# A hybrid decoder layer on one core: the first FFN's first part leaves raw, operand sums move to POOL, and a block's down products go behind

## The chip, the cores and the metric

One Trainium2 chip, one of its cores. The metric is the device time of one execution in microseconds, the median over runs. TensorE (PE) multiplies and has a separate loader of weights (PEld); VectorE (DVE), ScalarE (ACT) and GpSimd (POOL) do the elementwise work; SyncE (SP) issues nearly all DMAs. TensorE's clock has two levels, 1.2 and 2.4 GHz, and the profile shows what was granted (PEclk, 1.00 is 2.4 GHz).

## The reference, cut to what matters

One decoder layer over 1024 prompt tokens and 64 sample tokens, 1088 columns in all. The change touches the first FFN:

```
rmsnorm(x, g) = x * rsqrt(mean(x*x) + 1e-6) * g
swiglu(x)     = (silu(x @ w_gate) * (x @ w_up)) @ w_down      # 1024 -> 2752 -> 1024
h = x + 0.5 * rmsnorm(swiglu(rmsnorm(x, g1)), g2)
u = rmsnorm(h, g3)          # then the projection u @ w_in, attention, a second FFN
```

## The kernel before, in words

**Layout and precision.** Features lie on the 128 partitions (8 blocks of 128 for 1024), tokens in columns. Every operand of TensorE is split into a high part (rounded by ScalarE, `split`, L194) and a low part (the rest, by VectorE, L195), and each product is three matmuls: high by high, high by low, low by high. FFN rows come in 22 blocks of 128, block 0 a half block (the tail). `GROUPS` (L30) makes 7 groups of them: [0,1], four of four blocks, [18,19] and [20,21].

**Two parts.** The first FFN runs as `f1a` over columns 0 to 511 and then `f1b` over 512 to 1087 (576 columns, chunks of 256 and 320). A part goes through the groups in order (`plan1`, L1653): group 0 by `job_first` (L520), groups 1 to 5 as "sevens", group 6 plain ("final"). After a group's gate and up products, four jobs (`job_down`, L637) multiply its hidden blocks by a quarter each of `w_down` and add the result into `y` (L511; the first group copies, L509).

**Sevens** (`seven`, `job_seven`, `sevens`). For a hidden block, gate and up together are a two by two block product over halves of the features and halves of the columns, done with seven products of half size instead of eight. It needs sums of weight blocks (`Sums.load`, L77, on POOL, with scratch) and sums of operand blocks: `sevens` (L620) subtracts quarters of the normalised `y` in place on VectorE (L630, eight subtracts), and splits each into operands. For `f1a` the scratch of the weight sums and of the products is `y1`, for `f1b` it is `y0`; the operand sums' splits lie in the other part's operand tiles (`flata`, `flatb`). Since `sevens` works in place in `y`, group 0's down products wait, in order of issue, for all of it (`need`, L640), before the tail weights `wt` are cast (L643, L644).

**End of a part.** Group 6's down jobs run by chunks and square each row block as it is finished (`square`, L269). `f.after` then starts `norm` (L351): statistics by a matmul with ones (L294), rows by a matmul with a diagonal (L343), eight scalar_tensor_tensors (L382), the residual added (L383) and the result stored to `h1`, squares again, statistics again, eight scalar_tensor_tensors for the next norm (L405). For `f1b` the result is split into operands (L411, L412). For `f1a` it is stored in DRAM as `u0` (`spill`, L408), because `y0` must become scratch; `olds` of `f1b` begins with `need(("u0", ...))` (L1662), and `next2` (L1648), after `f1b`'s sevens, has `again` (L1637) load `u0` into `y0` and split it. The projection's first unit needs it (`hook2`, L1674).

**What sets the order.** Jobs are issued in one list (`work`, L694); `Feed` (L98) loads weights two requests ahead and splits up to three ahead (`NW`). Work beside TensorE's is a generator; `tick` (L210), called after each few matmuls with their estimated time, steps `quick` and the first of `side`. The framework's scheduler then reorders instructions within each engine by readiness in its own model, except where `keep` asks for program order.

Of the kernel before, what the change touches and what calls it, by code (L numbers as in the profile page):

```python
# [8 lines left out]
F32 = mybir.dt.float32  # L9
# [4 lines left out]
ALU = mybir.AluOpType  # L14
# [4 lines left out]
P = 128  # L19
D = 1024  # L20
KB = 8
# [136 lines left out]
class Part:  # L158
# [4 lines left out]
    room = None  # L163


class Step:
# [184 lines left out]
    def norm(self, y, y0, c0, n, pool, post=None, pre=None, v=None, key=None, spill=None):  # L351
# [49 lines left out]
        for k in range(KB):  # L401
# [4 lines left out]
            if spill is not None:  # L406
                if k % 4 == 3:
                    nc.sync.dma_start(spill[:, k - 3:k + 1, c0:c0 + n], y[:, k - 3:k + 1, c0 - y0:c0 - y0 + n])  # L408
                continue
# [5 lines left out]
    def ffn(self, w_gu, w_dn, f):  # L415
# [64 lines left out]
        def down(g, d2, w, wt, c0, n, first, s0=0, sums=None):  # L480
            hi, lo = w
            o = slice(c0 - f.b0, c0 - f.b0 + n)
            pds = {}
            seq = []
            for part in ((g[:-1], g[-1:]) if len(g) > 1 else (g,)):
                for e in range(2):
                    for hb in part:
                        i = g.index(hb)
                        hh, hl = hid[hb]
                        s = slice(s0 + (2 * i + e) * P, s0 + (2 * i + e) * P + P)  # L490
                        x, xl = hh[:, o], hl[:, o]
                        if hb == HB_TAIL:
                            ops = [(wt[:, e * P:e * P + P], x), (hi[:, s], xl)]
                        else:
                            ops = [(hi[:, s], x), (hi[:, s], xl), (lo[:, s], x)]
                        seq.append((e, i, ops))
            for e, i, ops in seq:
                if e not in pds:
                    pds[e] = self.mm(n)
                for j, (a, b) in enumerate(ops):  # L500
                    nc.tensor.matmul(pds[e], a, b, start=(i == 0 and j == 0), stop=(i == len(g) - 1 and j == len(ops) - 1))  # L501
                self.tick(len(ops) * n * COL)

            def evac():
                for e in range(2):
                    k = 2 * d2 + e
                    yk = f.y[:, k, c0 - f.y0:c0 - f.y0 + n]
# [4 lines left out]
                    if sums is not None:  # L512
                        self.square(yk, k, n, f.N, sums)
# [1364 lines left out]
```

## Time and profile before

| what | value |
|---|---|
| median of 3 runs | 2407.62 us (2406.84 to 2412.11) |
| the profiled execution | 2410.29 us, its span 2408.5 us, mean granted clock 0.976 |
| PE busy | 2270.2 us (94%) |
| PEld busy | 2039.4 us (85%) |
| DVE busy | 1616.2 us (67%) |
| ACT busy | 1041.9 us (43%) |
| POOL busy | 693.6 us (29%) |
| DMA | 362.71 MB, 151 GB/s over the span |

The chain of waits that ended last goes mostly through TensorE's matmuls (17% of the span by its rows). Matmuls overlap, so a mean duration is longer than the step from one to the next; the step is read from a stretch's instructions and its length. Times are microseconds from the start of the span.

### The profile page before, as it was taken

Reading aid. Unit: us, or ns where it says so; the run is one execution under the profiler, and the core shown is the slowest. Engines: PE = TensorE matmul, PEld = TensorE weight load, DVE = VectorE, ACT = ScalarE, POOL = GpSimd, SP = SyncE. Lnnn points to the kernel's source line nnn. Section 1 sums busy time; section 2 is a strip of 40 time slices with the busy share of each in tenths; the row PEclk is TensorE's granted clock in tenths of the full one; section 3 lists DMA queues with packets and bytes.
Section 4 is the critical chain, followed back from the end, with each engine's and each line's share of the span. In section 5 each row is a group of like instructions: output and inputs, shape, how many; then the busy total and the mean of one; then the engine's idle time right before and its main releaser. Section 6 shows DMA issues by size and latency. Waiting matters only on the chain. (4 is left out here: it accounts for less than half of the span.)

```text
span 2408.5 us, 41672 instructions
## 1 busy us (share of the span) xinstructions
PE 2270.2 (94%) x15584; PEld 2039.4 (85%) x15584; DVE 1616.2 (67%) x2881; ACT 1041.9 (43%) x1786; POOL 693.6 (29%) x650
## 2 busy tenths in 40 slices
PE   6999999699999999999999999998997999999997
PEld 5888978699999978989998566667786988999997
DVE  6887868678776575676556233339785696778765
ACT  5444335334433355665454222226465644344332
POOL 3444413333441021011125453631010224334402
PEclk8999999799999999999999999999998999999998
DMA  4332332533222367665356998865555545333212
GB/s 140 110 95 93 91 126 63 168 94 98 87 87 82 108 205 242 208 197 160 116 185 207 334 315 295 298 185 161 165 165 158 176 133 162 101 93 94 80 58 91
DMA packets 203627, 362.71 MB, mean 151 GB/s; under 512 B 28257, under 2 KB 103842, under 8 KB 203426
## 3 DMA queue, kind: packets, MB, share of 16 engines
q1 hardware_dynamic: 191762, 321.76, 42.8%
q0 software_dynamic: 11664, 38.28, 4.6%
q8 instruction: 124, 2.03, 0.3%
q14 instruction: 77, 0.63, 0.1%
HBM read 314.17 MB, written 45.79 MB: 149 GB/s over the span
## 5 line engine op out<-in xcount | busy, mean ns | idle before, releaser
L265 PE MATMUL mm<-ua,wh 128*128 128x512 f32 (+2 forms) x1712 | 461.8, 358 | 9.1 <-ACT wh L194 5.8
L195 DVE TENSOR_TENSOR wl<-wr,wh 128x1024 fp32r<-128x1024 f32 (+1 forms) x249 | 290.6, 1167 | 145.7 <-ACT wh L194 136.9
L194 ACT CAST wh<-wr 128x1024 fp32r<-128x1024 f32 (+1 forms) x249 | 244.9, 985 | 285.4 <-PE mm L265 110.9
L501 PE MATMUL mm<-hl,wh 128*128 128x320 f32 (+2 forms) x1072 | 349.5, 327 | 7.3 <-DVE hl L195 5.8
L265 PEld LDWEIGHTS mm<-ua,wh 128*128 128x128 f32 (+1 forms) x1712 | 295.7, 194 | 66.0 <-issue 22.4
L501 PE MATMUL mm<-hh,wh 128*128 128x256 f32 (+2 forms) x1024 | 335.9, 331 | 15.5 <-ACT hh L583 6.4
L501 PE MATMUL mm<-hh,wl 128*128 128x256 f32 (+2 forms) x1024 | 332.2, 325 | 0.9 <-DVE wl L195 0.9
L265 PE MATMUL mm<-ub,wh 128*128 128x320 f32 (+1 forms) x1472 | 312.0, 307 | 10.1 <-ACT ub L194 7.9
L265 PE MATMUL mm<-ua,wl 128*128 128x512 f32 (+1 forms) x848 | 296.3, 351 | 2.2 <-DVE wl L195 2.2
L556 PE MATMUL mm<-ub,wh 128*128 128x288 f32 (+1 forms) x1440 | 281.4, 291 | 8.4 <-ACT wh L194 8.4
L265 PEld LDWEIGHTS mm<-ub,wh 128*128 128x128 f32 x1472 | 239.3, 193 | 13.9 <-ACT ub L194 8.1
L556 PEld LDWEIGHTS mm<-ub,wh 128*128 128x128 f32 x1440 | 229.9, 191 | 8.9 <-ACT wh L194 8.9
L511 DVE TENSOR_TENSOR y<-y,mm 128x256 f32<-128x256 f32 (+2 forms) x296 | 142.1, 505 | 137.4 <-PE mm L501 136.4
L501 PEld LDWEIGHTS mm<-hh,wh 128*128 128x128 f32 x1024 | 194.5, 191 | 38.2 <-ACT hh L583 8.6
L556 PE MATMUL mm<-ua,wh 128*128 128x288 f32 (+1 forms) x1152 | 226.2, 293 | 0.0
L501 PEld LDWEIGHTS mm<-hl,wh 128*128 128x128 f32 x1072 | 206.7, 193 | 21.7 <-DVE hl L195 6.7
L265 PE MATMUL mm<-ub,wl 128*128 128x256 f32 (+1 forms) x720 | 215.7, 300 | 0.5 <-DVE wl L195 0.5
L89 POOL TENSOR_TENSOR y<-y,wz 128x512 f32<-128x512 f32 x54 | 71.8, 1329 | 490.5 <-DVE wl L195 473.5
L556 PE MATMUL mm<-ub,wl 128*128 128x288 f32 (+1 forms) x720 | 210.1, 292 | 0.0
L501 PEld LDWEIGHTS mm<-hh,wl 128*128 128x128 f32 x1024 | 195.7, 191 | 15.0 <-DVE wl L195 2.6
L556 PEld LDWEIGHTS mm<-ua,wh 128*128 128x128 f32 x1152 | 185.0, 191 | 0.5
L265 PEld LDWEIGHTS mm<-ua,wl 128*128 128x128 f32 x848 | 164.0, 194 | 23.8 <-DVE wl L195 4.2
(290 smaller groups left out, 4420.0 us busy)
## 6 DMA issues: line engine op xcount, KB each, us to landing
wr<-in_wd SPq DMA_DIRECT2D x68, 512.0 KB
wr<-in_wgu SPq DMA_DIRECT2D x64, 512.0 KB
pr<-in_ck SPq DMA_DIRECT2D x112, 256.0 KB
wz<-in_wgu SPq DMA_DIRECT2D x108, 256.0 KB
wr<-in_win SPq DMA_DIRECT2D x50, 512.0 KB
wr<-in_wout SPq DMA_DIRECT2D x32, 512.0 KB
y<-in_wgu SPq DMA_DIRECT2D x54, 256.0 KB
wx<-in_wgu SPq DMA_DIRECT2D x54, 256.0 KB
```

Source lines behind the costliest of these rows:

```text
L89: nc.gpsimd.tensor_tensor(out=out, in0=a, in1=b, op=op)
L194: self.keep(self.nc.scalar.copy(hi, src))
L195: self.keep(self.nc.vector.tensor_tensor(out=lo, in0=src, in1=hi.bitcast(F32), op=ALU.subtract))
L265: nc.tensor.matmul(out, a, x[:, k, o:o + n], start=(k == 0 and j == 0), stop=(k == KB - 1 and j == len(ops) - 1))
L501: nc.tensor.matmul(pds[e], a, b, start=(i == 0 and j == 0), stop=(i == len(g) - 1 and j == len(ops) - 1))
L511: nc.vector.tensor_tensor(out=yk, in0=yk, in1=pds[e], op=ALU.add)
L556: nc.tensor.matmul(ps, a, x, start=(k == 0 and j == 0), stop=(k == KB // 2 - 1 and j == len(ops) - 1))
```

## The change

1. `f1a` is `raw`: group 6's down products run on one chunk of 512, no squares; `away` stores `y0` unnormalised in DRAM (`y0d`). `olds` of `f1b` waits for nothing. After `f1b`'s sevens, `next2` loads it back in two chunks and starts the whole `norm` (squares, residual, pre-norm, operands) for each. `spill`, `u0` and `again` go.
2. In `f1b` group 5 is plain ("mid") instead of sevens, between `next2` and group 6.
3. The operand sums of `sevens` run on POOL (all three parts with sevens). They are started ahead of the tail's product, in `f1b` at the first chunk instead of the last; `need(("sevens", ...))` moves from `job_down` into the evacuation `evac_down`. `f1b`'s first chunk needs the norm of both its chunks.
4. In groups of sevens, `downs` takes two quarters of `w_down` in one job (one chunk) or one quarter with both chunks, four banks in all, and runs all products of the earlier blocks for the four banks before those of the last block. Where three banks of the pool are in use the fourth comes from `px`.

```diff
 class Part:
     room = None
+    raw = early = False
+    def bank(self, i, n):
+        if i < self.nmm:
+            return self.mm(n)
+        return self.px.tile([P, 512], F32, name=self.uid("mx"), tag="mx", bufs=1)[:, :n]
 ...
+        def downs(g, parts, first):
+            pds = {}
+            last = g[-1:] if len(g) > 1 else g
+            for hbs in ((g[:-1], last) if len(g) > 1 else (g,)):
+                for part in parts:
+                    d2, w, wt, c0, n, s0, sums = part
 ...
+                    if hbs is last:
+                        self.soon(lambda part=part: evac_down(pds, first, *part))
+
+        def evac_down(pds, first, d2, w, wt, c0, n, s0, sums):
+            if first and f.room:
+                self.need(("sevens", f.b0))
+            for e in range(2):
 ...
+                if sums is not None and not f.raw:
+                    self.square(yk, k, n, f.N, sums)
+            if sums is not None and d2 == 3:
+                if f.raw:
+                    f.after(c0, n)
+                    return
 ...
         def job_first(g, ws):
                 f.first(i)
+                if f.room and i == (0 if f.early else len(f.firsts) - 1):
+                    self.beside(sevens(), True)
                 tail(ws[0], c0, n)
                 if i == len(f.firsts) - 1:
                     self.feed.free(1, NW)
-                if f.room and i == len(f.firsts) - 1:
-                    self.beside(sevens(), True)
 ...
-                    nc.vector.tensor_tensor(out=out[:, h], in0=p[:, h], in1=q[:, h], op=ALU.subtract)
+                    nc.gpsimd.tensor_tensor(out=out[:, h], in0=p[:, h], in1=q[:, h], op=ALU.subtract)
 ...
         def job_down(g, d2, w, chunks, final):
-            if f.room and HB_TAIL in g:
-                self.need(("sevens", f.b0))
 ...
-            cs = [c for c in CH if chunks[0][0] <= c[0] < sum(chunks[-1])] if fin else chunks
-            for d2 in range(4):
+            cs = [c for c in CH if chunks[0][0] <= c[0] < sum(chunks[-1])] if fin and not f.raw else chunks
+            ds = []
+            if kind == "sevens":
+                ds = list(range(3 - len(cs)))
+                jobs.append(([[w_dn[d2][:, 2 * P * g[0]:2 * P * (g[-1] + 1)]] for d2 in ds],
+                             lambda *ws, g=g, ds=ds, cs=cs: downs(g, [(d2, w, None, *c, 0, None) for d2, w in zip(ds, ws) for c in cs], False), 0))
+            for d2 in range(len(ds), 4):
 ...
-        def again():
 ...
+        def away(c0, n):
+            for k in range(0, KB, 4):
+                nc.sync.dma_start(self.y0d[:, k:k + 4, c0:c0 + n], y0[:, k:k + 4, c0:c0 + n])
         def next2():
             self.kept = False
-            self.need(("u0", CH[1][0]))
-            self.beside(again(), True)
+            for c0, n in CH[:2]:
+                nc.sync.dma_start(y0[:, :, c0:c0 + n], self.y0d[:, :, c0:c0 + n])
+                self.beside(self.norm(y0, 0, c0, n, F, (1, A["xT"], self.h1), 2, None, "p"))
+        def plan1(chunks, then, m):
+            return ([(G[0], chunks, "first")] + [(g, chunks, "sevens") for g in G[1:m]] + [(None, [([], then, 0)], "jobs")]
+                    + [(g, chunks, "mid") for g in G[m:6]] + [(G[6], chunks, "final")])
+        f1a = Part(..., firsts=CH[:2], first=first1, plan=plan1(MID[:1], next1, 6), raw=True, after=away)
+        f1b = Part(..., first=lambda i: self.need(("f1", CH[3][0])), early=True, plan=plan1(MID[1:], next2, 5), ...)
-        sums(f1b, flata, lambda: y0, lambda: self.need(("u0", CH[1][0])))
+        sums(f1b, flata, lambda: y0)
```

## Rows read from the trace of the kernel before

**Rows 1.** The profile page, its second part: TensorE's busy share in each of 40 slices of the span, in tenths, and the clock that it was granted.

```profile
PE   6999999699999999999999999998997999999997
PEclk8999999799999999999999999999998999999998
```

**Rows 2.** Stretches of the first FFN. Columns: the stretch (us from the span's start), its length, then busy time and instructions of PE, PEld, DVE, ACT and POOL, granted clock, DMA share, GB/s.

```profile
44.00:52.00 8.00, 0.92 (x2) 0.83 (x3) 7.88 (x15) 4.09 (x8) 0.00 (x0) 0.71 0.33 98
357.00:386.00 29.00, 27.10 (x121) 21.80 (x122) 20.23 (x37) 14.01 (x30) 8.00 (x9) 0.94 0.25 73
386.00:405.00 19.00, 14.36 (x94) 13.26 (x94) 17.28 (x35) 10.69 (x26) 8.31 (x10) 0.84 0.31 98
405.00:426.00 21.00, 20.91 (x157) 20.65 (x155) 18.62 (x40) 12.76 (x28) 6.04 (x7) 0.98 0.21 62
426.00:463.00 37.00, 20.54 (x100) 19.03 (x100) 26.70 (x58) 13.93 (x33) 8.17 (x10) 0.68 0.63 194
463.00:469.00 6.00, 0.53 (x3) 0.52 (x3) 0.53 (x1) 2.08 (x4) 4.96 (x4) 0.85 0.37 124
469.00:479.00 10.00, 10.00 (x60) 10.00 (x59) 6.04 (x9) 3.40 (x5) 6.05 (x4) 0.75 0.34 105
751.00:773.00 22.00, 22.00 (x169) 22.00 (x168) 15.90 (x26) 11.05 (x15) 1.29 (x1) 1.00 0.20 56
773.00:790.00 17.00, 14.13 (x98) 12.79 (x97) 15.12 (x31) 6.12 (x9) 1.20 (x1) 1.00 0.58 178
790.00:815.00 25.00, 25.00 (x190) 25.00 (x189) 9.82 (x18) 6.05 (x11) 0.00 (x0) 1.00 0.22 64
815.00:830.00 15.00, 13.75 (x102) 13.28 (x101) 12.85 (x25) 8.76 (x18) 3.76 (x4) 1.00 0.35 113
```

**Rows 3.** What TensorE waited for from 0 to 62 us: us in total, times, longest.

```profile
PE mm L501 <- DVE wt L644: 7.6, 1, 7.6
```

**Rows 4.** The same from 62 to 345 us, the first part's five groups of sevens.

```profile
PE mm L501 <- ACT hh L583: 6.3, 4, 1.6
```

**Rows 5.** The same from 400 to 476 us.

```profile
PE nrows L343 <- DVE dg L336: 6.8, 3, 4.4
PE mm L556 <- ACT wh L194: 5.5, 1, 5.5
PE mm L501 <- DVE hl L195: 5.1, 1, 5.1
PE ncol L294 <- DVE ss L279: 4.7, 2, 4.1
```

**Rows 6.** VectorE in order of time at the first part's start: start, duration, engine, line, operation, out<-in, shapes, count.

```profile
36.69 1.05 DVE L630 TENSOR_TENSOR y<-y 128x512 f32<-128x512 f32 x1
...
43.32 1.28 DVE L630 TENSOR_TENSOR y<-y 128x512 f32<-128x512 f32 x2
...
45.12 1.28 DVE L195 TENSOR_TENSOR ub<-y,ub 128x512 fp32r<-128x512 f32 x2
46.33 1.88 DVE L630 TENSOR_TENSOR y<-y 128x512 f32<-128x512 f32 x3
48.13 1.88 DVE L195 TENSOR_TENSOR ub<-y,ub 128x512 fp32r<-128x512 f32 x3
49.94 0.67 DVE L630 TENSOR_TENSOR y<-y 128x512 f32<-128x512 f32 x1
50.64 0.29 DVE L644 CAST wt<-wl 64x256 fp32r<-64x256 f32 x1
```

**Rows 7.** VectorE's costliest groups from 400 to 465 us: line, operation, out<-in, shapes, count, busy us, mean ns of one, idle before.

```profile
L382 DVE SCALAR_TENSOR_TENSOR y<-y,gain,nrows 128x256 f32<-128x256 f32 x16 | 7.1, 470 | 0.0
L279 DVE TENSOR_TENSOR ss<-ss,sq 128x256 f32<-128x256 f32 x14 | 6.6, 476 | 0.7 <-ACT sq L275 0.5
L405 DVE SCALAR_TENSOR_TENSOR y<-y,gain,nrows 128x256 f32<-128x256 f32 x16 | 6.4, 476 | 2.0 <-PE nrows L343 2.0
L630 DVE TENSOR_TENSOR y<-y 128x576 f32<-128x576 f32 x8 | 6.0, 750 | 0.0
```

**Rows 8.** Two stretches of back-to-back matmuls, columns as in the second group: down products of 512 columns in the first part (306 to 323), and products of 288 columns in the second FFN (2042 to 2073).

```profile
306.00:323.00 17.00, 17.00 (x74) 13.69 (x74) 8.86 (x10) 3.50 (x4) 2.49 (x3) 1.00 0.19 63
2042.00:2073.00 31.00, 31.00 (x236) 31.00 (x235) 30.06 (x36) 15.26 (x20) 19.84 (x12) 1.00 0.28 94
```

**Rows 9.** Weight sums on POOL and weight splits on VectorE from 62 to 345 us, the columns of the seventh group. Of each engine two forms of one shape; the first of each pair is the one that runs while the other engine is at its own.

```profile
L89 POOL TENSOR_TENSOR y<-wx,y 128x512 f32<-128x512 f32 x17 | 33.7, 1985 | 0.9 <-DMA wx<-in_wgu 0.9
...
L89 POOL TENSOR_TENSOR y<-y,wz 128x512 f32<-128x512 f32 x17 | 22.0, 1292 | 162.9 <-DVE wl L195 162.9
...
L195 DVE TENSOR_TENSOR wl<-wz,wh 128x1024 fp32r<-128x1024 f32 x18 | 33.9, 1882 | 1.8 <-ACT wh L194 1.8
...
L195 DVE TENSOR_TENSOR wl<-y,wh 128x1024 fp32r<-128x1024 f32 x17 | 20.7, 1220 | 3.3 <-ACT wh L194 3.3
```

**Rows 10.** Two loads and the first instruction that waited for each, from the timeline: y1 (2304 KB), then the first piece of the second part's weight sums (256 KB).

```profile
345.70 0.57 SPq L1633 DMA_DIRECT2D y<-in_xT  x1
...
354.53 0.72 ACT L275 ACTIVATE ss<-y 128x256 f32<-128x256 f32 x2 [5.37 <-DMA y<-in_xT]
...
459.72 0.34 SPq L86 DMA_DIRECT2D y<-in_wgu  x1
...
463.66 1.26 POOL L89 TENSOR_TENSOR y<-y,wz 128x512 f32<-128x512 f32 x1 [10.51 <-DMA y<-in_wgu]
```

More of the change, by code (lines that the diff above doesn't have):

```diff
@@ L349, in need, with norm @@
             self.step_side(True)
-    def norm(self, y, y0, c0, n, pool, post=None, pre=None, v=None, key=None, spill=None):
+    def norm(self, y, y0, c0, n, pool, post=None, pre=None, v=None, key=None):
         nc = self.nc
@@ L480, in down @@
         def down(g, d2, w, wt, c0, n, first, s0=0, sums=None):
-            hi, lo = w
-            o = slice(c0 - f.b0, c0 - f.b0 + n)
+            downs(g, [(d2, w, wt, c0, n, s0, sums)], first)
+        def downs(g, parts, first):
             pds = {}
[L484 to L507, printed above, removed]
-                    if first:
-                        nc.scalar.copy(yk, pds[e])
-                    else:
-                        nc.vector.tensor_tensor(out=yk, in0=yk, in1=pds[e], op=ALU.add)
-                    if sums is not None:
-                        self.square(yk, k, n, f.N, sums)
-                if sums is not None and d2 == 3:
-                    v = []
-                    self.beside(self.stat(sums, n, f.N, v), True)
-                    self.beside(f.after(c0, n, v))
@@ new lines, in evac_down @@
+        def evac_down(pds, first, d2, w, wt, c0, n, s0, sums):
+            if first and f.room:
+                self.need(("sevens", f.b0))
+            for e in range(2):
+                k = 2 * d2 + e
+                yk = f.y[:, k, c0 - f.y0:c0 - f.y0 + n]
+                if first:
+                    nc.scalar.copy(yk, pds[d2, c0, e])
+                else:
+                    nc.vector.tensor_tensor(out=yk, in0=yk, in1=pds[d2, c0, e], op=ALU.add)
+                if sums is not None and not f.raw:
[4 more added lines that the diff above has]
+                    return
+                v = []
+                self.beside(self.stat(sums, n, f.N, v), True)
+                self.beside(f.after(c0, n, v))
@@ L1648, in next2 @@
         def next2():
             self.kept = False
-            self.need(("u0", CH[1][0]))
-            self.beside(again(), True)
-        def plan1(chunks, then):
-            return [(G[0], chunks, "first")] + [(g, chunks, "sevens") for g in G[1:6]] + [(None, [([], then, 0)], "jobs"), (G[6], chunks, "final")]
-        f1a = Part(b0=0, n=HALF, y=y0, y0=0, H=F, N=F, tanh=False, firsts=CH[:2], first=first1, plan=plan1(MID[:1], next1),
-                   after=lambda c0, n, v: self.norm(y0, 0, c0, n, F, (1, A["xT"], self.h1), 2, v, "u0", self.u0))
@@ L1658, in whole @@
-        f1b = Part(b0=HALF, n=H1N, y=y1, y0=HALF, H=F, N=F, tanh=False, firsts=CH[2:], first=lambda i: self.need(("f1", CH[2 + i][0])),
-                   plan=plan1(MID[1:], next2),
+            for c0, n in CH[:2]:
[4 more added lines that the diff above has]
+                    + [(g, chunks, "mid") for g in G[m:6]] + [(G[6], chunks, "final")])
@@ L1660, in whole @@
+        f1a = Part(b0=0, n=HALF, y=y0, y0=0, H=F, N=F, tanh=False, firsts=CH[:2], first=first1, plan=plan1(MID[:1], next1, 6), raw=True, after=away)
+        f1b = Part(b0=HALF, n=H1N, y=y1, y0=HALF, H=F, N=F, tanh=False, firsts=CH[2:], first=lambda i: self.need(("f1", CH[3][0])), early=True,
+                   plan=plan1(MID[1:], next2, 5),
                    after=lambda c0, n, v: self.norm(y1, HALF, c0, n, F, (1, A["xT"], self.h1), 2, v, "p"))
         sums(f1a, flatb, lambda: y1)
-        sums(f1b, flata, lambda: y0, lambda: self.need(("u0", CH[1][0])))
+        sums(f1b, flata, lambda: y0)
```

34 lines of the change are left out of this document (20 added, 14 removed).

## The prediction, on record before the result

> **What bounds the kernel now.** I read the page first [rows 1]: TensorE is busy in nearly every slice, so only the slices where it is not can pay. Counted from 0, the digits 6 stand in slices 0 and 7 and both lie in the first FFN (a slice is 60 us; slice 7 is 421 to 482 us), and in both the granted clock falls too. Next come the stretches [rows 2], cut at the stages of the first FFN: its first part (512 columns) ends with group 6, plain, 357 to 405 us; its second part (576 columns) starts at 405. Full speed there is known from plain stretches: 190 matmuls of 256 and 320 columns in 25 us, 0.132 us each [rows 2]; 512 columns take 17/74 = 0.230 us and 288 columns 31/236 = 0.131 us [rows 8]. Against that: the down products of group 6 (386 to 405) take 19 us where 48 of 512 columns would take 11; the down products of the second part's group 0 (426 to 463), 80 matmuls worth 80 x 0.132 = 10.5 us, take 37; then TensorE all but stands from 463 to 469. Third, who is waited for: at 400 to 476 almost all of TensorE's waits are on VectorE, and one of 5.5 us on a weight cast [rows 5]. VectorE's groups there [rows 7] show why: normalising the first part (32 scalar_tensor_tensor, 13.5 us, and square sums, 6.6 us) and the operand sums (L630, 6.0 us) stand ahead of the `hl` subtract that group 0 needs. The weight cast waits for a longer thing: y0 serves as scratch for the second part's weight sums, and they can't be loaded before the normalised rows have been written away; the load was issued at 459.72 and POOL saw it at 463.66 [rows 10]. Last, two smaller places: 7.6 us at the kernel's first down product [rows 3] and 6.3 us, 1.6 at each of four group ends, in the first part [rows 4].
>
> **The change, term by term** (us; minus is gained).
>
> **A, first part's start.** TensorE waits 7.6 us for `wt` (L644) [rows 3]; from 44 to 52 it is busy for 0.92 us, and the clock falls [rows 2]. VectorE's order [rows 6]: six operand sums (3.8 us) and five splits (3.2 us) run from 43.3 to 50.6 and the 0.3 us cast comes behind them. The change puts eight sums on POOL, and `need(sevens)` goes from ahead of `wt` to ahead of the first evacuation, so the cast and the matmuls are issued before the remaining sums. What is late next: the evacuation overwrites y, so it waits for POOL's chain. No row shows an operand sum on POOL; the nearest are POOL's weight sums of the same 512 elements, 1.29 us alone and 1.99 in the form that meets VectorE [rows 9]. Eight are 10.3 to 15.9 us, against 0.6 us each on VectorE. At 1.29, begun where VectorE begins now (36.7), the chain ends about 47 to 48 us; VectorE's last sum ends at 50.6 [rows 6]. I take the low price, since POOL has nothing else there: -6; ends -8 and +3 (the last worked out under the rivals).
>
> **B, down products of the last block behind.** Now 18 matmuls (18 x 0.23 = 4.1 us) cover the last block's silu, product and split, and 1.6 us is missing. With two quarters in one job there are 36, 8.3 us of cover. Four group ends: -6.3 at best [rows 4]. Against it: the next quarter needs a bank that was finished only nine matmuls before, about 2 us, for an evacuation that VectorE does in about 0.6 if nothing is ahead of it; a job holds two of three weight buffers, so the fourth quarter's split is issued later. I take -6, ends -6.5 and -2. In the other two FFN parts with such groups two chunks already give this cover: TensorE is busy 31.00 of 31 us [rows 8], so 0.
>
> **C, group 6's down products, first part.** Squares and statistics go (raw), chunks are 512 wide. 48 x 0.230 = 11.0 against 19 us. The matmul time itself hardly moves; what goes is VectorE's queue. I leave 1.5 us, because the second half's own pre-normalisation still ends here: -6.5, ends -8 and -3.
>
> **D, second part's group 0, gate and up.** 144 matmuls x 0.132 = 19.0 of now 21; operand sums go to POOL and start at the first chunk, the first part's norm is gone: -1.5, ends -2 and +3 (the first chunk now waits, in order of issue, for the norm of both).
>
> **E, its down products.** 37 to 10.5 us. VectorE loses 26 us of work [rows 7] from the stretch 400 to 465; left are splits and evacuations. POOL's sums, 8 x 1.29 x 576/512 = 11.6 us (17.9 at the slow price), have D's 19.5 us of cover before an evacuation needs them; without it, E loses one for one. -26, ends -26.5 and -18.
>
> **F, first product of the sevens.** Now 5.5 us of wait [rows 5] and 60 matmuls in 10 us at granted clock 0.75 where 7.9 would do [rows 2]: 7.6 us. After: the chain from group 6's end is evacuation 1.5, raw spill of 2.1 MB at the rate of the 2.36 MB load (345.70 to 354.53 [rows 10], 267 GB/s) 7.9, weight load 3.9 (459.72 to 463.66 [rows 10]), POOL's adds, cast and first product about 5: 18.3 us. Cover is D and E, 30. Even behind 17.9 us of operand sums on POOL the adds end at 23. The spill's two DMAs stand in SP's queue and hold back the loads issued behind them for 8 us; those are the quarters of `wd`, not wanted for 20. -5, since adds, spill and splits meet in one place: ends -7.6 and +6.
>
> **G, second part's end.** Group 5 turns plain. Now its sevens and downs take 22 + 17 us, group 6 (plain) 25 + 15 [rows 2]: 79. Two plain groups are 2 x 40 = 80: +1. Seven products cost 22, eight 25, but in the 17 us TensorE stood for 2.9 us. The two full norms of the first part come here: reload 2.1 MB (the SP instruction waits until the last sevens free the scratch, and the loads for group 5 stand behind it), squares, residual, squares, pre-norm; eight x loads (256 KB) and four h1 stores move here with them. VectorE is free for 15 of 25 us in a plain group's gate and up [rows 2], and the reload can land in group 4's downs, so I cost the norms at nothing; were the cover gone they cost what they did at 386 to 405, some 8 us per overlap of norm and downs. Ends -1 and +12.
>
> Sum: -6 -6 -6.5 -1.5 -26 -5 +1 = **-50**. The profiled execution took 2410.3 us, so 2360; it lies 2.7 us above the median of the runs, 2407.6, which I don't subtract.
>
> **A rule against the change.** Where POOL and VectorE meet, the trace shows both longer: POOL's 512-element sum 1.29 and 1.99, VectorE's 1024-element subtract 1.22 and 1.88 [rows 9]. The Trainium skill ("SBUF — State Buffer", Who interferes with whom) says more: a VectorE instruction with two SBUF inputs and a GpSimd one that reads SBUF block each other fully, whichever comes second, for the whole instruction. By that rule each operand sum would cost VectorE up to its own 1.29 us, and the sum would be near the first rival's, 2369; the rows show about half of that per meeting.
>
> **Rivals.**
> 1. *The operand sums block VectorE after all* (0.13). Mechanism in this kernel: eight sums at 1.99 are 15.9 us from 36.7, ending at 52.6 to 53.5 where the last one now ends at 50.6 [rows 6], and each meeting adds 0.66 to a VectorE subtract (8 x 0.66 = 5.3, what was moved away). Evacuations and the first product come 3 us later than now: A is +3, not -6. 2369. For: [rows 9]; against: in A POOL's sums meet mainly PSUM readers and ScalarE.
> 2. *The weights come late* (0.12): spill, weight traffic and sums queue up beyond the 30 us of cover; F is +6 with a new fall of the clock. 2371. Against: 12 us of slack.
> 3. *The norms crowd the plain groups* (0.13): G is +12. 2371. For: 386 to 405 now; against: twice the time and two chunks per weight.
> 4. *The down order gives nothing* (0.07): a bank or weight wait takes the place of the 1.6 us; B is 0. 2366. This is also where the change would not do what it says.
> 5. *Slower* (0.04): the stall moves whole to the projection. Its first unit needs the normalised first part. Now two such norms fill the stretches 405 to 463 [rows 2, 7], 58 us beside all else; with the reload (8) I take 60 to 65. The scratch is free some 105 us before the projection (25 of downs, 80 of G). So up to 40 us of delay in the reload cost nothing, beyond that it counts one for one, and only past 95 is the whole gain gone. With the reload held to the end of group 6 all 60 us are exposed: 2360 + 60 = 2420. It needs the reload to start more than two groups late, behind SP's weight loads, and nothing in [rows 10] holds a load that long.
>
> **The numbers.** The forecast case has 0.51 and by its terms' own ends 2351 to 2368; rivals 1 to 4 reach to 2371, and two of them together to 2382. Below, all best ends give 2351, and some 5 us more if the 29 us of 357 to 386, where 96 x 0.23 = 22 would do, shrink with VectorE's load [rows 2]. Range **2346 to 2382**. A measurement of this kernel tells about 0.2% (4.8 us) from no change; every case but the fifth is beyond that. Faster 0.94, same 0.02, slower 0.04.
>
> **What would show it.** In the profile after: slice 7 at 9 tenths with PEclk 9; no wait of TensorE above 2 us between 400 and 440; first product of the second part's sevens some 48 us earlier than 468; `hh` waits (1.6) gone from the first part; the wait for `wt` under 2 us; L630 on POOL at 1.3 to 1.5 us each; the two parts' plain groups at 40 us each, the norms' scalar_tensor_tensors inside them, and the projection starting without a wait. Wrong would be: a POOL wait on an L630 successor that TensorE inherits (rival 1), TensorE waiting for `wh` behind POOL's adds (2), waits on VectorE in the plain groups or at the projection's first unit (3, 5).

## The result and the profile after

The changed kernel has a median of 2384.46 us (2383.17 to 2385.52) beside 2407.23 (2405.45 to 2412.11) for the kernel before: ratio 0.9902, 95% interval 0.9885 to 0.9919. It is faster by 22.8 us, where 50 were forecast, and lies 2.5 us above the top of the range. Its profiled execution took 2383.47 us (span 2381.6), 26.8 less than that of before.

The page after, TensorE's share and granted clock in 40 slices (a slice is 59.5 us), answering [rows 1]:

```profile
PE   6999998999999989999998999999997989999997
PEclk9999999999999999999999999999997999999998
```

Slice 7, the forecast's main place, reads 9 in both rows. Four slices that read 9 before now read 8 (6, 14, 21 and 32); the one that matters below is slice 32 (1905 to 1965 us, in the second FFN).

Stretches of the changed kernel, columns as in [rows 2]: group 6's down products of the first part, the second part's group 0 (gate and up, then down), its first sevens; then group 4's downs, groups 5 and 6 (plain) up to the projection.

```profile
376.00:390.00 14.00, 11.04 (x46) 7.81 (x45) 10.26 (x17) 5.90 (x11) 12.02 (x11) 1.00 0.35 87
390.00:411.00 21.00, 19.47 (x146) 19.06 (x144) 18.75 (x21) 9.00 (x17) 13.31 (x9) 1.00 0.48 169
411.00:424.00 13.00, 12.06 (x82) 10.88 (x82) 6.71 (x11) 10.88 (x28) 0.45 (x1) 1.00 0.47 142
424.00:434.00 10.00, 10.00 (x78) 10.00 (x77) 6.90 (x9) 3.94 (x7) 5.65 (x4) 1.00 0.26 84
...
724.00:750.00 26.00, 25.07 (x187) 24.47 (x187) 21.87 (x52) 11.50 (x25) 6.98 (x10) 1.00 0.41 119
750.00:776.00 26.00, 25.71 (x194) 25.48 (x194) 19.98 (x46) 10.52 (x24) 9.60 (x11) 1.00 0.49 150
776.00:792.00 16.00, 14.36 (x103) 13.45 (x102) 14.41 (x28) 9.28 (x19) 3.99 (x4) 1.00 0.35 108
```

The 37 us of group 0's down products [rows 2] are 13, the 6 us behind them, in which TensorE all but stood, are gone, and the first sevens run 78 matmuls in 10 us at clock 1.00, where it was 60 at 0.75.

The best view for what follows is a table of landmarks: the same matmul is found in each trace, and the time from one to the next is compared, in one profiled execution of each version. Stages: (1) to the first sevens product; (2) to the last sevens product of the first part's five groups; (3) to the second part's first gate product, that is group 5's down products, group 6 and term C; (4) to its first sevens product, D, E and F's wait; (5) to the last sevens product of its group 4; (6) to the projection, that is group 4's down products, groups 5 and 6, G; (7) to the sample tokens' attention; (8) to its last product; (9) to the second FFN's second part's first sevens product; (10) to its last sevens product; (11) to the last product of all.

```
                       1     2     3     4     5     6     7     8     9    10    11
before               61.9 281.9  61.0  63.7 256.6 104.6 485.6 496.5 216.7 307.6  61.8
after                58.9 274.7  56.2  34.0 257.1 110.6 485.6 496.3 226.4 309.3  61.8
f3_vector            58.9 274.6  56.9  33.9 257.0 110.5 482.5 495.4 217.3 309.7  62.2
all_vector           61.3 274.7  55.6  32.9 257.2 110.6 485.3 495.7 216.8 309.5  61.8
pairs_one            59.1 274.7  56.6  34.0 254.1 110.2 484.0 497.8 225.4 307.9  62.1
pairs_one_f3_vector  59.5 274.7  57.2  34.0 254.1 110.5 484.0 497.5 217.8 308.4  61.9
before_pool          63.1 282.0  66.6  60.0 256.2 104.3 485.3 499.3 224.8 307.4  62.3
no_norm              59.8 274.7  59.2  34.0 257.0 104.1 488.7 496.9 225.1 309.5  62.2
f3_double            58.8 274.7  55.4  34.0 257.1 110.5 485.1 494.7 221.2 309.5  61.8
f3_pinned            59.2 274.7  57.6  34.0 257.0 110.9 484.2 495.8 231.4 308.5  61.8
before_pairs         61.8 274.6  62.3  64.8 256.2 105.5 484.5 503.0 216.5 307.6  62.7
raw_alone            61.5 282.1  54.1  33.4 254.0 110.1 488.0 506.6 217.0 307.6  61.8
five_sevens          58.8 274.7  58.0  33.9 257.0 125.1 489.6 507.3 224.7 309.3  61.8
f3_early_double      59.5 274.6  58.3  33.9 257.0 110.7 485.7 506.0 221.1 309.5  61.8
f3_pinned_double     58.9 274.6  56.7  34.0 257.0 110.5 485.7 504.7 223.0 310.3  62.2
first_sums_pool      59.5 274.6  58.0  34.2 254.2 110.2 488.7 503.0 216.9 308.1  62.5
```

In stages 2, 4, 5 and 6 versions with the same code there repeat within about 1 us, in stage 10 within 1.8; stages 3, 7 and 8 vary by more (raw_alone and the changed kernel have the same code in 7 and 8; ten versions with the same code in stage 3 have 55.4 to 59.2 there). The last six versions ran on other chips, on which the kernel before too took longer (2420.06 and 2418.82); their traces have it in stage 8; their ratios to it compare, their times don't.

Waits of TensorE in the changed kernel, 0 to 59 us (answering [rows 3]), 334 to 424 ([rows 5]), 424 to 681, and 1773 to 2000; columns as in [rows 3]. From 59 to 334 the four `hh` waits of [rows 4] are gone.

```profile
PE mm L272 <- POOL ua L415: 2.7, 1, 2.7
PE mm L511 <- DVE wt L658: 1.4, 1, 1.4
...
PE mm L511 <- ACT hh L195: 2.0, 1, 2.0
...
PE mm L511 <- DVE y L525: 2.3, 3, 0.8
...
PE mm L511 <- DVE sg L440: 6.4, 1, 6.4
PE mm L572 <- ACT wh L195: 3.8, 1, 3.8
```

The forecast waits are gone or short. New ones are those for POOL's `ua`, for the cast `hh`, for a bank (`y`), and the largest, for `sg`, in the other FFN. (L272 answers to L265 of before, L511 to L501, L572 to L556, L195/L196 to L194/L195, L415 to L412, L440 to L437, L646 to L630, L658 to L644, L525 to L511.)

**The wait of 6.4 us.** VectorE of the changed kernel, in order of time, columns as in [rows 6]; `sg` (L440) is what TensorE waits for:

```profile
1924.54 0.69 DVE L434 SCALAR_TENSOR_TENSOR sg<-sg,mm 128x512 f32<-128x512 f32 x1 [0.18 <-ACT sg L433]
1925.15 3.04 DVE L415 TENSOR_TENSOR ub<-y,ub 128x320 fp32r<-128x320 f32 x2
1928.11 2.45 DVE L196 TENSOR_TENSOR wl<-wr,wh 128x1024 fp32r<-128x1024 f32 x1
1930.48 3.28 DVE L196 TENSOR_TENSOR ua<-y,ua 128x576 fp32r<-128x576 f32 x2
1934.52 1.93 DVE L196 TENSOR_TENSOR ua<-y,ua 128x576 fp32r<-128x576 f32 x1 [0.77 <-POOL ub L415]
1936.38 0.67 DVE L440 SCALAR_TENSOR_TENSOR sg<-sg,mm 128x512 f32<-128x512 f32 x1
```

and POOL beside it:

```profile
1924.75 4.72 POOL L646 TENSOR_TENSOR y<-y 128x576 f32<-128x576 f32 x3
1929.43 1.84 POOL L415 TENSOR_TENSOR ub<-y,ub 128x320 fp32r<-128x320 f32 x1
1931.35 1.79 POOL L646 TENSOR_TENSOR y<-y 128x576 f32<-128x576 f32 x1
1933.10 1.38 POOL L415 TENSOR_TENSOR ub<-y,ub 128x320 fp32r<-128x320 f32 x1
1934.44 5.64 POOL L646 TENSOR_TENSOR y<-y 128x576 f32<-128x576 f32 x3
```

From the end of the tanh product (L434, 1925.2) to `sg` 11.2 us pass. In f3_vector, the version below whose sums are on VectorE, the same stretch is:

```profile
1919.33 0.69 DVE L434 SCALAR_TENSOR_TENSOR sg<-sg,mm 128x512 f32<-128x512 f32 x1 [0.18 <-ACT sg L433]
1919.93 1.57 DVE L415 TENSOR_TENSOR ub<-y,ub 128x320 fp32r<-128x320 f32 x2
1921.42 1.89 DVE L196 TENSOR_TENSOR wl<-wr,wh 128x1024 fp32r<-128x1024 f32 x1
1923.24 2.08 DVE L646 TENSOR_TENSOR y<-y 128x576 f32<-128x576 f32 x3
1925.24 0.68 DVE L440 SCALAR_TENSOR_TENSOR sg<-sg,mm 128x512 f32<-128x512 f32 x1
...
1927.58 0.74 DVE L196 TENSOR_TENSOR ua<-y,ua 128x576 fp32r<-128x576 f32 x1
```

It takes 5.2 us. Of the 5.9 more, 5.0 are the same instructions lasting longer (3.04 for 1.57, 2.45 for 1.89, and 5.21 for three splits at 0.74 to 0.75), 0.9 are the order (three splits and 0.8 idle instead of three sums). Moving eight sums of 0.75 us off VectorE made VectorE later. (In f3_vector POOL is not idle there either: its own two subtracts L415 run from 1920.08 to 1922.23.) TensorE meanwhile, from 1928 to 1939 us, columns as in [rows 2]:

```profile
1928.00:1939.00 11.00, 3.49 (x23) 2.92 (x21) 10.06 (x8) 3.96 (x6) 10.84 (x7) 0.72 0.17 48
```

It is busy for 3.49 of 11 us and its granted clock is 0.72 over the stretch; in [rows 2] it was 0.71 and 0.68 over the stretches with such stops.

### The profile page after: what moved, and what is told of

It is laid out like the page before. It is cut to its first block, busy times and chain, and to the rows that moved or that the text cites. A ratio compares the mean times of both kernels' runs of the same rounds, so it can differ in the third digit from the quotient of the medians.

```text
span 2381.6 us, 41583 instructions
## 1 busy us (share of the span) xinstructions
PE 2265.0 (95%) x15560; PEld 2031.4 (85%) x15560; DVE 1606.7 (67%) x2837; ACT 1037.8 (44%) x1794; POOL 729.8 (31%) x674
## 5 line engine op out<-in xcount | busy, mean ns | idle before, releaser
L272 PE MATMUL mm<-ua,wh 128*128 128x512 f32 (+2 forms) x1712 | 462.9, 358 | 10.9 <-ACT wh L195 4.2
L196 DVE TENSOR_TENSOR wl<-wr,wh 128x1024 fp32r<-128x1024 f32 (+1 forms) x253 | 299.9, 1186 | 136.5 <-ACT wh L195 134.3
L195 ACT CAST wh<-wr 128x1024 fp32r<-128x1024 f32 (+1 forms) x253 | 249.3, 986 | 291.6 <-PE mm L272 107.2
L272 PEld LDWEIGHTS mm<-ua,wh 128*128 128x128 f32 (+1 forms) x1712 | 296.6, 194 | 68.7 <-issue 22.4
L272 PE MATMUL mm<-ub,wh 128*128 128x320 f32 (+2 forms) x1600 | 337.4, 306 | 11.8 <-ACT ub L195 8.4
L511 PE MATMUL mm<-hh,wh 128*128 128x320 f32 (+2 forms) x990 | 328.2, 333 | 17.4 <-DVE sg L440 6.4
L511 PE MATMUL mm<-hl,wh 128*128 128x256 f32 (+2 forms) x1038 | 337.5, 326 | 0.6 <-DVE hl L196 0.5
L511 PE MATMUL mm<-hh,wl 128*128 128x320 f32 (+2 forms) x990 | 322.2, 326 | 0.9 <-DVE wl L196 0.9
L272 PE MATMUL mm<-ua,wl 128*128 128x512 f32 (+1 forms) x848 | 296.7, 351 | 1.4 <-DVE wl L196 1.4
L572 PE MATMUL mm<-ub,wh 128*128 128x288 f32 (+1 forms) x1392 | 270.8, 290 | 3.8 <-ACT wh L195 3.8
L272 PEld LDWEIGHTS mm<-ub,wh 128*128 128x128 f32 (+1 forms) x1600 | 259.1, 192 | 15.8 <-ACT ub L195 8.6
L272 PE MATMUL mm<-ub,wl 128*128 128x320 f32 (+1 forms) x784 | 234.2, 299 | 0.3 <-DVE wl L196 0.3
L525 DVE TENSOR_TENSOR y<-y,mm 128x256 f32<-128x256 f32 (+2 forms) x283 | 138.1, 514 | 133.2 <-PE mm L511 132.7
L572 PEld LDWEIGHTS mm<-ub,wh 128*128 128x128 f32 x1392 | 221.6, 190 | 4.0 <-ACT wh L195 4.0
L511 PEld LDWEIGHTS mm<-hh,wh 128*128 128x128 f32 x990 | 187.5, 190 | 42.2 <-DVE y L525 8.6
L572 PE MATMUL mm<-ua,wh 128*128 128x288 f32 (+1 forms) x1104 | 215.0, 290 | 0.0
L511 PEld LDWEIGHTS mm<-hl,wh 128*128 128x128 f32 x1038 | 197.2, 190 | 14.5 <-DVE hl L196 1.5
L572 PE MATMUL mm<-ub,wl 128*128 128x288 f32 (+1 forms) x696 | 202.4, 291 | 0.0
L511 PEld LDWEIGHTS mm<-hh,wl 128*128 128x128 f32 x990 | 187.8, 190 | 15.9 <-DVE wl L196 2.6
L272 PEld LDWEIGHTS mm<-ua,wl 128*128 128x128 f32 x848 | 164.4, 194 | 22.2 <-DVE wl L196 2.7
L572 PEld LDWEIGHTS mm<-ua,wh 128*128 128x128 f32 x1104 | 175.8, 190 | 0.5
```

The source lines that it names most:

```text
L195: self.keep(self.nc.scalar.copy(hi, src))
L196: self.keep(self.nc.vector.tensor_tensor(out=lo, in0=src, in1=hi.bitcast(F32), op=ALU.subtract))
L272: nc.tensor.matmul(out, a, x[:, k, o:o + n], start=(k == 0 and j == 0), stop=(k == KB - 1 and j == len(ops) - 1))
L511: nc.tensor.matmul(pds[key], a, x, start=(i == 0 and j == 0), stop=(i == len(g) - 1 and j == len(ops) - 1))
L525: nc.vector.tensor_tensor(out=yk, in0=yk, in1=pds[d2, c0, e], op=ALU.add)
L572: nc.tensor.matmul(ps, a, x, start=(k == 0 and j == 0), stop=(k == KB // 2 - 1 and j == len(ops) - 1))
```

## The experiments

Medians are of two to ten runs; the ratio is to the kernel before on the same chip.

**1. Second FFN's sums back on VectorE.** f3 is that FFN's second part.

```diff
-nc.gpsimd.tensor_tensor(out=out[:, h], ...
+(nc.vector if f.last else nc.gpsimd).tensor_tensor(out=out[:, h], ...   # f3 has last=True
```

> The changed kernel, but the operand sums of the second FFN's second part go back to VectorE. Theory (POOL's sums slow VectorE just where the last block's gate of the second FFN's first part is evacuated): the 6.4 us wait of TensorE for sg, the 1.1 us for hh and about 2 us at the following start go, 2384.5 becomes 2374 to 2377. Rival (the wait belongs to the shifted order of the whole, not to the sums): 2383 to 2386, the wait stays above 4 us.

2373.5 us, ratio 0.985 (0.9832 to 0.9868): 11 us off the changed kernel. Stage 9 is 217.3 instead of 226.4 and the wait for `sg` 0.5. The sums on POOL were the loss there.

**2. All sums on VectorE** (L646 `nc.vector` for every part).

> The changed kernel with all three sets of operand sums on VectorE; the moved wait for them, the raw first part and the order of down products stay. If POOL's sums help at the two starts in the first FFN as the forecast had it (6 us at the first, cover at the second), this is 2380 to 2388 although the 9 us in the second FFN come back. If they cost there too (VectorE instructions lengthen, the pre-norm's low halves wait on POOL), 2370 to 2376, and the first part's sevens start at 56 to 59 us or earlier.

2374.64, 0.9855 (0.9835 to 0.9875). Stage 1 loses 2.4 (61.3, where at most 59 was expected), the rest of the first FFN loses nothing. POOL's sums are worth 2.4 us in one place; the moved `need` by itself takes the wait for `wt` from 7.6 to 6.1 us and stage 1 down by 0.6.

**3. Four-bank jobs only in the one-chunk part.**

```diff
-if kind == "sevens":
+if kind == "sevens" and len(cs) == 1:
```

> The changed kernel, but the four-bank job only where a part has one chunk (the first part); the two parts with two chunks keep one job per quarter. Theory (four banks filled at once make the next quarter wait for its bank, 0.8 us at each of three group ends in the first FFN's second part and about 0.4 at each in the second FFN): 2379.5 to 2382. Rival (these waits are filled by what is late next): 2383.5 to 2386.

2376.97, 0.9863 (0.9846 to 0.988). Stages 5 and 10 fall by 3.0 and 1.4 and the waits for `y` (L525) are gone from 424 to 680; that is 4.4 of the 7.5 by medians, the rest is in no stage of the change.

**4. The kernel before with its sums on POOL and nothing else.**

> The kernel before with nothing changed but the operand sums on POOL. Theory (sums on POOL slow VectorE and delay POOL's own pre-norm work): a wait of 5 to 8 us appears at the end of the second FFN's first part, the first part's start gains at most 3, the jam at 426 to 463 hardly changes: 2407 to 2414, slower or the same. By the forecast's term A alone it would gain 6: 2399 to 2403.

2423.46 beside 2410.49, 1.0047 (1.0033 to 1.0062): slower, by more than expected, where term A alone would have given -6. Stage 1 is +1.2, 3 +5.6, 4 -3.7, 9 +8.1, and the wait of 6.4 us for `sg` is there. Alone the move costs at each of the three places where the sums run, two of them by little; in all three VectorE and POOL normalise at the same time.

**5, 6. POOL work that nobody waits for.** Both are f3_vector with eight more POOL subtracts of 512 elements that write scratch; in f3_double they read the sums, in f3_early_double the operands of the same rows.

```diff
+n2 = f.H.tile([P, 2, 256], F32, name=self.uid("dbl"), tag="dbl", bufs=1)
+nc.gpsimd.tensor_tensor(out=n2, in0=out[:, h, :256], in1=out[:, h, :256], op=ALU.subtract)                # f3_double
+nc.gpsimd.tensor_tensor(out=n2, in0=uh[:, i:i + 2, :256]..., in1=ul[:, i:i + 2, :256]..., op=ALU.subtract) # f3_early_double
```

> The operand sums of the second FFN's second part on VectorE (2373.5 so), and beside each a POOL subtract of 512 elements that reads VectorE's sum and writes scratch that nobody reads. Sharing (VectorE's instructions get longer while POOL reads SBUF, whoever waits for whom): a wait for sg or hl of 3 us or more returns at the end of the second FFN's first part, VectorE's subtracts there last 1.5 to 2.5 us, 2377 to 2385. Order (VectorE and ScalarE stand in their queues behind casts and splits that wait for POOL's slower sum): nothing waits for these, so 2372 to 2376 and no wait above 1 us.

> The version with the second FFN's last sums on VectorE, and eight POOL subtracts of 512 elements that read the operands uh and ul of the same rows (as early as those are split) and write scratch that nobody reads: POOL works beside VectorE where the changed kernel's operand sums did, but no VectorE instruction has to wait for the result. Sharing theory: VectorE's instructions ahead of sg stretch as in the changed kernel and TensorE's wait for sg at the end of the last down products is 4 to 6 us again: 2380 to 2385. Order theory (the splits that wait for POOL's sums stand ahead of sg in VectorE's queue): the wait stays under 1.5 us: 2373 to 2377. This holds only if the doubles do run in the 20 us ahead of that wait, which the trace must show.

2376.54, 0.9856, and ratio 0.9881 (0.986 to 0.9902), both without a wait for `sg` above 0.5. They don't decide: the scheduler put the doubles behind the critical stretch, from 1950.83 and from 1963.88 us, long after `sg` (1927.44 and 1940.52). They do show that POOL work whose result nobody reads costs: stage 9 is 221.2 and 221.1 instead of 217.3.

**7. The same, pinned into the stretch.** Fourteen subtracts of 320 elements on POOL, between its own L415 subtracts of that pre-norm, in program order.

```diff
+if k % 2 and key == "f2" and c0 == CH[3][0]:
+    self.tc.keep_in_program_order(ins)          # the L415 subtract
+    a = xh[:, k - 1, o:o + n].bitcast(F32)
+    dbl = pool.tile([P, 320], F32, ...)
+    for _ in range(2 if k == 1 else 4):
+        self.tc.keep_in_program_order(nc.gpsimd.tensor_tensor(out=dbl, in0=a, in1=a, op=ALU.subtract))
```

> The version with the second FFN's last sums on VectorE, and fourteen POOL subtracts of 320 elements between POOL's own low-half subtracts of the same pre-norm, pinned there, reading operands that are done and writing scratch that nobody reads: POOL is busy beside VectorE in the stretch ahead of sg, VectorE's order is that of the version without them, and nothing waits for the result. Sharing theory: VectorE's instructions between the tanh's product and sg (5.2 us in the version without, 11.2 in the changed kernel, of which 5.0 are longer instructions and 0.9 the splits in the queue) stretch again, to 8 to 10 us, and TensorE's wait for sg is 2.5 to 5 us. Order theory: they stay 5.2 to 6 us and the wait is about 0.5 us. Time: 2374 by order, 2377 to 2380 by sharing.

Ratio 0.988 (0.986 to 0.99). VectorE, then POOL, of this version (L440 is here the tanh product, L446 is `sg`, L652 the sums, L421 the doubles):

```profile
1933.53 0.69 DVE L440 SCALAR_TENSOR_TENSOR sg<-sg,mm 128x512 f32<-128x512 f32 x1 [0.18 <-ACT sg L439]
1934.14 1.56 DVE L415 TENSOR_TENSOR ub<-y,ub 128x320 fp32r<-128x320 f32 x2
1935.62 1.74 DVE L196 TENSOR_TENSOR wl<-wr,wh 128x1024 fp32r<-128x1024 f32 x1
1937.28 3.82 DVE L652 TENSOR_TENSOR y<-y 128x576 f32<-128x576 f32 x3
1941.02 0.68 DVE L446 SCALAR_TENSOR_TENSOR sg<-sg,mm 128x512 f32<-128x512 f32 x1
```

```profile
1933.70 4.24 POOL L421 TENSOR_TENSOR dbl<-ub 128x320 f32<-128x320 f32 x4
1937.90 1.39 POOL L415 TENSOR_TENSOR ub<-y,ub 128x320 fp32r<-128x320 f32 x1
1939.26 5.28 POOL L421 TENSOR_TENSOR dbl<-ub 128x320 f32<-128x320 f32 x4
```

The order is that of f3_vector and nothing waits for the doubles; the three sums take 3.82 instead of 2.08, the stretch from the tanh product to `sg` 6.8 instead of 5.2, TensorE's wait for `sg` is 2.1 and stage 9 223.0. So sharing is real, and it is smaller here than expected.

How it works shows in the instructions one by one (the rows above merge neighbours). In the changed kernel's stretch six VectorE subtracts began while a POOL subtract was in progress:

```
elements   began     POOL's ended   it ended   after POOL's   lasts alone
320        1925.15   1926.19        1926.54    0.35           0.48
320        1926.46   1927.83        1928.18    0.35           0.48
1024       1928.11   1929.47        1930.55    1.08           1.22
576        1930.48   1931.27        1931.89    0.62           0.75
576        1931.81   1933.14        1933.76    0.61           0.75
576        1934.52   1935.85        1936.46    0.61           0.75
```

Each ended a fixed time after POOL's, 0.13 to 0.14 us less than it lasts alone: it waited until POOL's instruction was done. In this version six such subtracts ended 0.35, 0.35, 1.08, 0.61, 0.62 and 0.61 after POOL's, and in f3_vector the second of the pair (0.35) and the weight split (1.08) did, behind POOL's own L415. The changed kernel's six last 10.7 us and would take 4.4 alone; of the 6.3 between, 1.3 are in f3_vector too, and the rest is the 5.0 above. So those 5.0 us are this waiting. They are fewer here because a double is short (0.72 alone, a 576-element sum 1.40), and what VectorE loses at a meeting is the rest of POOL's instruction.

**8. Sums pinned behind POOL's earlier work** in the second FFN's second part.

```diff
+ins = nc.gpsimd.tensor_tensor(out=out[:, h], ...
+if f.last:
+    self.tc.keep_in_program_order(ins)
```

> The changed kernel with its sums on POOL, but those of the second FFN's second part are pinned behind what POOL was given before, so that they run in that part's own group 0. Both theories of the loss have it at the place where the sums run, not at POOL as such: the 6.4 us wait at the end of the first part goes; group 0 and the first sevens have 19 us of gate and up as cover for 8 x 1.57 = 12.6 us of sums: 2374 to 2378. If the cover does not do, up to 5 us come back at that part's down products: 2379 to 2382.

2386.32, 0.9895 (0.9879 to 0.9912): a miss, 8 us above the better of the two ranges. The wait for `sg` of L440 is gone, but the sums start at 1959.01 and TensorE waits from 1920 to 2005 for what comes after them:

```profile
PE mm L511 <- ACT y L523: 7.2, 1, 7.2
PE mm L511 <- DVE sg L442: 5.1, 1, 5.1
PE nrows L350 <- DVE dg L343: 3.0, 1, 3.0
```

The first evacuation needs the whole chain of sums (`need` in `evac_down`); on POOL it is either beside VectorE's pre-norm or too late.

**9. Both repairs**: experiments 1 and 3 together.

> Both repairs together: four-bank jobs only in the first part, operand sums of the second FFN's second part on VectorE. If they are independent, 2384.5 - 11.0 - 7.5 = 2366; part of the second repair's gain lies in the second FFN, where both act, so 2366 to 2369. Clearly above 2370 would mean that one of the two gains was chance of the order.

2368.8 (2366.3 to 2371.88), 0.982 (0.9804 to 0.9837): the fastest version, ahead of the changed kernel by 15.7.

**10. The same with sums on POOL in the first part alone** (`nc.gpsimd if f.raw else nc.vector`, four-bank jobs as in 3).

> The changed kernel with four-bank jobs only in the first part and operand sums on POOL only there; the other two parts' sums on VectorE. If POOL's sums pay only at the first start (-2.3) and cost where VectorE's pre-norm runs beside them, this is the sum of all repairs: one or two us below the version with both repairs (ratio 0.982), so 0.980 to 0.982. Rival: in the first FFN's second part POOL's sums shorten VectorE's queue as forecast; then this is 1 to 3 us above it, 0.983 or more.

0.9847 (0.9824 to 0.9871), which overlaps 9. Stages 3 and 4 together are 92.2 against 91.2: where the second part's sums run makes no difference that these runs can tell.

**11. Without the first part's norms** (raw rows are reloaded, stored to `h1` and split; left out are squares, statistics, residual and the pre-norm).

> The changed kernel without the first part's normalisation: its raw rows are loaded back, stored to h1 as they are and split; squares, statistics, residual and pre-norm are left out. From the end of group 4 to the projection the changed kernel takes 84.6 us where before took 79.2. Theory (the norms' own matmuls, 32 at 0.09 us, and VectorE's queue make this difference): 80 to 82 us here, whole time 2378 to 2382. Rival (the plain group itself): 84 to 85, 2383 to 2386.

2381.94, 0.9878 (0.9858 to 0.9898). Stage 6 falls from 110.6 to 104.1: the norms cost 6.5 us there. (Its stage 3 was 3 longer.)

**12. Group 5 as sevens again** (`plan1(MID[1:], next2, 6)`), the norms beside group 6 only.

> The changed kernel with the second part's group 5 as sevens again, so that the two norms of the first part have only group 6 (40 us) beside them. If the two plain groups are needed as cover (such norms filled 58 us beside all else in the kernel before), some 15 to 20 us lie bare ahead of the projection: 2397 to 2405. Rival: the norms cost what their matmuls cost wherever they stand, and the plain group was paid for nothing: 2380 to 2383, a few us faster than the change.

0.9979 (0.9963 to 0.9994). Stage 6 is 125.1, 14.5 more than with the plain group. TensorE from 731 to 808 us:

```profile
PE ncol L301 <- DVE ss L286: 7.7, 2, 6.7
PE mm L511 <- DVE y L525: 4.7, 4, 3.0
PE nrows L350 <- DVE dg L343: 2.2, 3, 1.7
```

The plain group is needed as cover.

**13, 14. Single parts.** before_pairs is the kernel before with part 4 in the first part alone; raw_alone is the changed kernel with sums on VectorE and without four-bank jobs.

> The kernel before with part 4 of the change alone, and that only in the first part (one chunk, two quarters of w_down in one job). If part 4's worth there is its own (four waits of 1.6 us for hh, and the clock), it gives 6 to 7.5 us: 2400 to 2402 beside 2407.2, and the hh waits of the first part's group ends are gone. Rival: it needs VectorE's evacuations to be undisturbed, which the rest of the change brings; then a wait for y comes in their place and the time is 2404 to 2407.

> The changed kernel with all operand sums on VectorE and without the four-bank jobs: only the raw first part, the plain group 5 and the moved wait are left (parts 1, 2 and the order of part 3). The kernel with all sums on VectorE but with four-bank jobs had 2374.6; those jobs gave 7.1 in the first part and cost 2.6 and 1.7 in the two others, so this should be 2376 to 2380, that is 27 to 31 of the 22.8 us net gain by itself, and the second part's sevens start 36 to 37 us earlier than before. Rival: the parts lean on each other (group 0's down products need the sums on POOL or the shorter first part); then it gives under 20: above 2387.

before_pairs 0.9974 (0.9959 to 0.9988), 6.3 us: stage 2 falls by 7.3, all four `hh` waits gone. raw_alone 0.9872 (0.9843 to 0.9901), 31 us: stage 3 -6.9, 4 -30.3, 5 -2.6, 6 +5.5. The raw first part (with the plain group 5 and the moved `need`) gives all of the gain by itself.

## Why the prediction was right and where it failed

Against the profiled execution, by the table's stages (before to after):

```
term                                    forecast   measured
A  first part's start                     -6         -3.0   stage 1
B  first part's group ends                -6         -7.2   stage 2
B  in the other two parts                  0         +3.0   stage 5;  +1.7 stage 10
C  group 6's down products                -6.5       -4.8   stage 3
D + E + F                                -32.5      -32.3   stage 4 -29.7, stage 5 -2.6
G  second part's end                      +1         +6.0   stage 6
   operand sums of the second FFN        not priced  +9.7   stage 9
sum                                      -50        -26.9
```

The last landmark is 26.9 us earlier as well; stages 7, 8 and 11 change by 0.2 in all. Stage 5 as a whole is +0.5; raw_alone, without four-bank jobs, gives its -2.6 (the clock that no longer falls), and pairs_one the +3.0.

None of the costed terms came out worse than its own bad end. What carried the time over the top of the range are the two places put at nothing, 9.7 us in the second FFN and 4.7 for B; without either it would lie inside.

**Right.** D, E and F are right in kind: the second part's first sevens start 44.6 us earlier, the weights come in time and the clock stays up. That their sum meets the forecast to 0.2 us is luck: D gave 0.4 of 1.5, E 23.7 of 26, and F 8.2 where 5 was taken. raw_alone shows that it needs neither POOL nor the four-bank jobs. B in the first part was right; the whole stop of 1.6 us went, and a little more.

**Failed: the step that moved the sums to POOL.** Its place was the sum's first term and D; all three parts' sums move, by the description of the change, and two were costed. The third, in the second FFN, is the largest miss, 9.7 us: f3_vector, which takes only that back, has 217.3 in stage 9. Rival 1 named the mechanism (POOL beside VectorE) and a price per meeting, 0.66 us, but looked at the first start only. The price was low: the six meetings of the table in experiment 7 cost 0.7 to 1.2 us each, 1.1 in the mean. "About half of that per meeting" was the error of reading: [rows 9]'s 1.88 is the mean of 18 splits of which 13 began during a POOL sum, and what each of those lost is the rest of that sum.

At the first start A gave half of its 6. The wait for `wt` fell as forecast, from 7.6 to 1.4, and the price of a sum was nearly right: the eight took 1.3 to 1.6 us each and ended at 47.4 (forecast: 47 to 48). What was wrong is "POOL has nothing else there": it had half of the pre-norm's subtracts. Nor did the sums meet "mainly PSUM readers": VectorE's two `ub` splits at 38.90 took 3.12 us, two such splits before 1.29. POOL of the changed kernel:

```profile
31.98 1.27 POOL L646 TENSOR_TENSOR y<-y 128x512 f32<-128x512 f32 x1 [2.73 <-DVE y L412]
...
41.43 1.17 POOL L415 TENSOR_TENSOR ua<-y,ua 128x256 fp32r<-128x256 f32 x1
42.56 4.88 POOL L646 TENSOR_TENSOR y<-y 128x512 f32<-128x512 f32 x3
```

The sums, ready early, stand between those subtracts; the last of these ends at 42.6 (37.2 in the kernel before), and TensorE waits 2.7 us for it, not for an evacuation. The same in C: the cast `hh` stood behind a cast that waited for POOL's sum, 2.0 us of TensorE. ScalarE, then POOL, of the changed kernel:

```profile
378.62 0.67 ACT L195 CAST ua<-y 128x576 fp32r<-128x576 f32 x1 [2.39 <-POOL y L646]
379.20 0.61 ACT L195 CAST hh<-sg 128x512 fp32r<-128x512 f32 x1
```

```profile
375.95 1.03 POOL L415 TENSOR_TENSOR ub<-y,ub 128x320 fp32r<-128x320 f32 x1 [6.48 <-ACT ub L414]
377.05 1.54 POOL L646 TENSOR_TENSOR y<-y 128x576 f32<-128x576 f32 x1
```

That is the wait queued behind a waiting instruction which the forecast did not follow (its signs of being wrong have it): a sum on POOL has a cast on ScalarE and a split on VectorE behind it, and both stand in queues in which TensorE's next operand comes later. How much of C's shortfall it is, stage 3 doesn't tell, since it varies; C's own stretch, from the first of the 48 down products to the second part's first gate product, does better. It took 19.3 before and takes 15.0 to 15.1 in the changed kernel and the nine other versions with the same code there, 13.8 in raw_alone and all_vector and 14.6 in first_sums_pool, all three with these sums on VectorE; 12.5 was forecast. So POOL's sums cost C 0.4 to 1.2 us; the rest is there without them, in raw_alone as waits for evacuations (2.1 us).

**Failed: B "so 0" in the two-chunk parts.** The cover was there already, so nothing was to be gained; the price, a bank reused nine matmuls after it was finished, was named for the first part and not carried over. It is 3.0 and 1.7.

**Failed in size: G.** "The norms at nothing": VectorE had the room, but TensorE itself runs the norms' statistics. Groups of the changed kernel from 707 to 792 us, columns as in [rows 7]:

```profile
L350 PE MATMUL nrows<-dg,ones 128*128 128x128 f32 x16 | 2.4, 273 | 0.0
L301 PE MATMUL ncol<-ones,ss 128*128 128x2 f32 x16 | 2.1, 235 | 0.3 <-DVE ss L286 0.3
```

They overlap with their neighbours: from the product ahead of such a run to the one behind it, less the usual 0.132 us, they take 3.5 us in all. With waits for `y` of 2.2 that is most of the 6.5 that no_norm gets back. In the kernel before, the first part's norms ran where TensorE was idle anyway (for 21 of the 56 us from 386 to 405 and 426 to 463 [rows 2]). Rival 3 (+12) had the place right; it takes the plain group away to get there (five_sevens).

## What to carry to other kernels

When work moves to an idle engine, cost it in every place where the same helper runs, and at each ask what that engine has queued there and which instruction of the other engines waits for the result in front of something urgent: its busy share (here 29%) says nothing about that. A mean over instructions that met the other engine and some that did not is no price of a meeting. A reordering that closes a gap in one shape can open one where there was none, so give it only to the shape that had the gap. Work hidden beside TensorE is only hidden if TensorE executes none of it.

## What the runs showed of the hardware

POOL and VectorE, both subtracting from SBUF, take turns by whole instructions. A VectorE subtract with both inputs in SBUF that began during a POOL subtract ended 0.35 (320 elements), 0.61 to 0.62 (576) or 1.08 us (1024) after it, 0.13 to 0.14 less than it lasts alone, in all six cases of the table in experiment 7. The kernel before already shows it: of its 50 weight splits of 1024 elements that began during a POOL tensor_tensor, 48 ended 1.08 or 1.09 us after that one. It holds the other way too: POOL's subtract at 1929.43, begun while the weight split was under way, took 1.84 instead of 0.88 and ended 0.72 us after it. A scalar_tensor_tensor with one input in PSUM kept its 0.67 to 0.69 in all 21 cases in which it met a POOL instruction in the changed kernel.

The Trainium skill ("SBUF — State Buffer", Who interferes with whom) states that a VectorE instruction with two SBUF inputs contends with a GpSimd one that reads SBUF, that one with at most one SBUF input, outside the two-port modes, does not, that the order of issue decides who blocks, and that it is an exclusive lock. These rows agree with all four: the one that began later waited for the other's whole instruction, by turns.
